# A hybrid decoder block in float32: the intra-chunk scores of a head pair issued in two runs instead of three, with the bonus product moved behind them

## The chip, the cores and the metric

The kernel runs on one core of one Trainium2 chip. The metric is the device time of one execution in microseconds (us). The core has five engines with instruction queues of their own: TensorE (PE, with its weight loads shown as PEld), VectorE (DVE), ScalarE (ACT), GpSimd (POOL) and SyncE (SP), which here only issues DMAs. Products land in PSUM, which has eight banks of 128 partitions by 512 float32.

## The reference, cut to what matters

One decoder layer over 528 positions (16 learned ones and 512 of input), 1024 channels, all in float32:

```
p   = h @ W_in                      # GLU columns | RWKV r,k,v + low-rank columns | 2 gates
A   = conv module: GLU -> causal depthwise conv(31) -> LayerNorm -> swish -> projection
Bm  = RWKV-7 time mixing (16 heads of 64) -> projection
y   = sigmoid(gA) * A + sigmoid(gB) * Bm
x   = LN(alpha * x + y @ W_o);  x = LN(alpha * x + ConvGatedMLP(x))

# RWKV-7, per head, state S (64 x 64):
S_t = S_{t-1} diag(decay_t) + (S_{t-1} a_t) b_t^T + v_t k_t^T ;  y_t = S_t r_t
o   = LN(y) + sum(r * k * r_k) * v          # the second term is the "bonus"
```

## The kernel before, in words

The recurrence is computed in 9 chunks of 64 positions (chunk 0 holds only the 16 learned positions), for two heads at a time, so that a pair of heads fills 128 partitions: head 0 lies on partitions 0 to 63, head 1 on 64 to 127. There are 8 such pairs, p = 0 to 7. For each pair the code has these stages; the string SCHEDULE writes their order by hand:

- K (`rkv`): the r, k and v columns of the input projection, 6 half-width products, each of 24 matmuls (three for each of 8 blocks, L172, L175, L176) into a bank of tag "g". ACT and DVE empty the bank (L225, L227). G (`glu`) and A (`gate`) are further such products and do not depend on the pair's recurrence.
- P (`prep`): the decays, then the two operands of the scores, AR (from r and k, L434 and L436) and BK (L437 to L470; its last step is the multiplication at L470, in two parts: chunks 0 to 4, then 5 to 8). Then the bonus: two products with a matrix of ones (L478) into two banks of tag "a", each read by DVE together with v into the tile bv (L479). Then the scores: for each chunk and each head a 128 x 128 product over that head's 64 partitions (L490). Then 8 scalings of AR in place on ACT (L498), and transposes of BK and v (L506, L510), again through banks of tag "a".
- S (`solve`): a triangular solve on DVE in 31 dependent steps (L560 to L570), fed from the scores through DMAs, with the depthwise convolution of another channel block put between the steps (L754, L762).
- C (`merge` and `chain`): the solved blocks are brought back, then the 9 chunks are run one behind the other on PE, ACT and DVE (L624, L643 to L660). F (`finish`): norm, bonus and output gate (L671 to L713); it is the last reader of bv (L704).

The scores are issued in three parts, chunk 0, chunks 1 to 4 and chunks 5 to 8. Each part takes two banks of tag "a", one for each head; DVE multiplies each bank by a causal mask into the tile Gt (L492). Each float32 product is two passes on PE, so a part of one chunk is 4 records in the trace and a part of four chunks 16.

PSUM banks are handed out by tag: "g" has 3 banks (K, G, A), "x" has 2 (chain and finish), "a" has 2 (prep), "m" has 1 (a small product of prep at L454, and two of merge at L606 and L611). A tile of a tag waits until one of the tag's banks is released by its last reader.

The order of instructions on each engine is fixed at build time by a planner that goes by priority, which is the order of the code unless a block stands in `with front()`, which gives its instructions the highest priority; `behind(b, a, why)` makes b follow a on the same engine without a semaphore. merge and chain stand in `front()`; prep does not.

The tiles AR, Gt, bv, BT and UV have two buffers each, so those of pair p become free when chain and finish of pair p-2 have read them.

Of the kernel before, what the change touches and what calls it, by code (L numbers as in the profile page):

```python
# [11 lines left out]
F32 = mybir.dt.float32  # L12
F32R = mybir.dt.float32r
AF = mybir.ActivationFunctionType
ALU = mybir.AluOpType
# [3 lines left out]
P = 128  # L19
# [7 lines left out]
NCH = 9  # L27
# [19 lines left out]
GW = 132  # L47
# [7 lines left out]
def hybrid_block(ctx: ExitStack, tc: tile.TileContext, a, out, dbg=None):  # L55
    nc = tc.nc
    V, S, G, TE = nc.vector, nc.scalar, nc.gpsimd, nc.tensor
# [5 lines left out]
    def pool(stack, name, side, **kw):  # L63
        return stack.enter_context(tc.tile_pool(name=name, bufs=1, side=side, reuse_waits="tile", **kw))

    front = tc.high_priority
# [4 lines left out]
    def behind(ins, first, why):  # L71
        tc.add_manual_dep(ins.ins, first.ins.name, mybir.DependencyInfo(mybir.DependencyClass.NoSync,
                                                                mybir.DependencyReason.DATA), reason=why)
# [8 lines left out]
    def bank(tag, bufs):  # L82
        return psp.tile([P, 512], F32, name="ps_" + tag, tag=tag, bufs=bufs)

    gbank = lambda: bank("g", 3)
    xbank = lambda: bank("x", 2)
    abank = lambda: bank("a", 2)
    mbank = lambda: bank("m", 1)
# [18 lines left out]
    cmask = cp.tile([P, P], F32, name="cmask")  # L107
# [79 lines left out]
    turn, turn_a = cycle((gbank, xbank, gbank, xbank, gbank)), cycle((gbank, abank, gbank, abank, gbank))  # L187
# [21 lines left out]
    sp = pool(ctx_a2, "scan", "left")  # L209
# [39 lines left out]
    with tc.tile_pool(name="start", bufs=1, side="right", reuse_waits="tile") as st:  # L249
# [88 lines left out]
        c0 = 43  # L338
        for i, n in ((1, 112), (2, 128), (3, 120), (4, 88), (5, 44)):
# [15 lines left out]
                    in1=taps[:, :, 1, :], op=ALU.add)  # L355
# [31 lines left out]
    def prep(p, r, k, v):  # L387
# [15 lines left out]
        for hf, (t0, t1) in enumerate(HALF):  # L403
# [9 lines left out]
            else:  # L413
# [16 lines left out]
        AR = sp.tile([P, NCH, P], F32, name="AR", bufs=2)  # L430
        BK = ra.tile([P, NCH, P], F32, name="BK", bufs=1)
# [7 lines left out]
                               in1=Ei[:, :, 1:65], op0=ALU.mult, op1=ALU.mult)  # L439
# [24 lines left out]
        for g0, g1, c0, c1 in ((0, 3, 0, 5), (3, 5, 5, NCH)):  # L464
            pt = abank()
            for i in range(g0, g1):
# [4 lines left out]
                            in1=pt[:, 0:64 * (c1 - c0)].rearrange("p (c t) -> p c t", t=64), op=ALU.mult)  # L471


        bv = sp.tile([P, NQ], F32, name="bv", bufs=2)
        for t0, t1 in QH:
            pt = abank()
# [2 lines left out]
            V.tensor_tensor(out=bv[:, t0 - Q0:t1 - Q0], in0=pt[:, :n], in1=v[:, 64 + OFF + t0:64 + OFF + t1],  # L479
                            op=ALU.mult)  # L480


        Gt = sp.tile([P, 2, NCH, GW], F32, name="Gt", bufs=2)
        G.memset(Gt.rearrange("p h c (two x) -> p (h c two) x", two=2)[:, :, 64:66], 0.0)
        for c0, c1 in ((0, 1), (1, 5), (5, 9)):
            pts = [abank(), abank()]
            for c in range(c0, c1):
                for h in range(2):
                    o = pts[h][:, P * (c - c0):P * (c - c0 + 1)]
                    TE.matmul(o, BK[64 * h:64 * h + 64, c, :], AR[64 * h:64 * h + 64, c, :], start=True, stop=True)  # L490
            for h in range(2):
                V.tensor_tensor(out=Gt[:, h, c0:c1, :].rearrange("p c (two x) -> p c two x", two=2)[:, :, :, 0:64],  # L492
                                in0=pts[h][:, 0:P * (c1 - c0)].rearrange("p (c two t) -> p c two t", two=2, t=64),
                                in1=cmask.rearrange("p (two t) -> p two t", two=2).unsqueeze(1).broadcast_to(
                                    [P, c1 - c0, 2, 64]), op=ALU.mult)

        for c in range(1, NCH):
            S.activation(out=AR[:, c, :], in_=AR[:, c, :], func=AF.Copy, scale=lc[:, c - 1:c])  # L498
# [327 lines left out]
    for step in SCHEDULE.split():  # L826
        what, p, q = step[0], int(step[1:2] or 0), int(step[2:] or -1)
        if what == "K":
            raw[p] = rkv(p)
        elif what == "P":  # L830
            prs[p] = prep(p, *raw.pop(p))
        elif what == "S":
            solved[p] = solve(prs[p], conv(q, cpads.pop(q)) if q >= 0 else ())
        elif what == "C":
            with front():
                merge(prs[p], *solved[p])
                ys[p] = chain(prs[p])
        elif what == "F":
            finish(prs[p], ys.pop(p))
        elif what == "G":  # L840
            cpads[p] = glu(p)
        elif what == "T":
            with back():
                for _ in conv(p, cpads.pop(p)):
                    pass
        elif what == "A":
            gate(gates.pop(0))
        elif what == "N":
            ctx_a1.close()
            rb, zh, zl, mean = conv_norm()  # L850
        elif what == "H":
            hold.append(mean)
# [27 lines left out]
    op = pool(ctx_o, "rout", "left")  # L880
# [119 lines left out]
    for j in range(2, NF):  # L1000
        c = j - 2
# [80 lines left out]
```

## Time and profile before

| | us |
|---|---|
| three runs: median (lowest to highest) | 1181.84 (1171.94 to 1184.82) |
| the profiled execution | 1175.08 |
| its span, first to last instruction | 1173.0 |
| PE busy / DVE busy / ACT busy in the span | 1121.2 / 862.9 / 567.5 |
| mean granted TensorE clock, share of full speed | 0.989 |

How to read the rows below: times are in us from the start of the span. An engine's busy time is the union of its instructions. In rows of the order of time, the first column is the start, the second the length, then engine, line, operation, output tile <- input tiles, shapes, and how many instructions were merged into the row. Matmuls overlap in the pipeline, so what one costs is the distance from start to start, not its length. In rows on waits, "A <- B: t, n, m" means that A's engine stood idle t us in n places, at most m at once, until B was done.

### The profile page before, as it was taken

The numbers are of one execution on the slowest core, as the hardware profiler recorded it, in microseconds if no ns is written. First come the engines' busy times: TensorE is split into PE (matmuls) and PEld (weight loads), VectorE is DVE, ScalarE is ACT, GpSimd is POOL, SyncE is SP. The second block draws the span as 40 slices with busy tenths as digits, with TensorE's granted clock in tenths as the row PEclk, the third lists the DMA queues.
The fourth block names the chain that finished last, engine by engine and source line by source line (L and its number), as shares of the span: only waits on it lengthen the run. The fifth ranks groups of instructions, "written<-read, shape, count | busy, mean of one in ns | idle before, by whom it ended". The sixth has DMA issues, their size and how long they took to land.

```text
span 1173.0 us, 22681 instructions
## 1 busy us (share of the span) xinstructions
PE 1121.2 (96%) x8718; PEld 1056.2 (90%) x8718; DVE 862.9 (74%) x2179; ACT 567.5 (48%) x1214; POOL 83.6 (7%) x242
## 2 busy tenths in 40 slices
PE   5999999999999999999987999999999999999997
PEld 4998989899898989989887999998999999998885
DVE  6598998889899998976586366697876666662228
ACT  5644456637556565665577433355434343441120
POOL 7001011101101110101000000000000000000000
PEclk9999999999999999999988999999999999999999
DMA  5333341333414143354432476531332323333321
GB/s 163 84 93 92 87 97 50 87 77 91 101 56 109 42 103 79 85 125 106 140 100 65 139 227 203 158 88 54 109 109 73 108 73 109 89 123 113 102 78 72
DMA packets 202438, 118.99 MB, mean 101 GB/s; under 512 B 50036, under 2 KB 186397, under 8 KB 202331
## 3 DMA queue, kind: packets, MB, share of 16 engines
q1 hardware_dynamic: 182992, 113.81, 34.6%
q10 hardware_dynamic: 17515, 3.17, 1.5%
q8 instruction: 68, 1.11, 0.4%
q0 software_dynamic: 1824, 0.57, 0.3%
q14 instruction: 39, 0.32, 0.1%
HBM read 102.24 MB, written 15.28 MB: 100 GB/s over the span
## 4 chain that ended last, share of the span: by engine, by line
PE 65%; DVE 7%; DMA 4%; ACT 3%; issue 2%; DVEq 0%; ACTq 0%; POOL 0%; SPq 0%; POOLq 0%
PE ps_x L624 7%; PE ps_g L175 6%; PE ps_g L176 6%; PE ps_g L172 6%; PE ps_g L182 4%; PE ps_g L183 4%; PE ps_g L184 4%; PE psf L1027 3%; PE psf L1026 3%; PE psf L1028 3%; PE ps_x L182 3%; PE ps_x L183 3%; PE ps_x L184 3%; ACT wh L153 1%; PE ps_a L490 1%
## 5 line engine op out<-in xcount | busy, mean ns | idle before, releaser
L172 PE MATMUL ps_g<-hhi,wh 128*128 128x256 f32 (+2 forms) x944 | 278.9, 296 | 2.6 <-DVE v L227 1.7
L175 PE MATMUL ps_g<-hhi,wl 128*128 128x256 f32 (+2 forms) x944 | 278.6, 295 | 0.0
L176 PE MATMUL ps_g<-hlo,wh 128*128 128x256 f32 (+2 forms) x944 | 278.0, 295 | 0.0
L154 DVE TENSOR_TENSOR wl<-wr,wh 128x1024 fp32r<-128x1024 f32 x151 | 182.6, 1220 | 96.8 <-ACT wh L153 96.5
L153 ACT CAST wh<-wr 128x1024 fp32r<-128x1024 f32 x151 | 158.2, 1049 | 128.9 <-PE psf L1027 73.4
L172 PEld LDWEIGHTS ps_g<-hhi,wh 128*128 128x128 f32 x944 | 180.5, 191 | 5.2 <-DVE v L227 2.2
L175 PEld LDWEIGHTS ps_g<-hhi,wl 128*128 128x128 f32 x944 | 180.1, 191 | 2.6 <-issue 0.6
L176 PEld LDWEIGHTS ps_g<-hlo,wh 128*128 128x128 f32 x944 | 180.3, 191 | 1.4 <-issue 0.4
L182 PE MATMUL ps_g<-hhi,wh 128*128 128x256 f32 (+1 forms) x424 | 120.0, 283 | 0.0
L183 PE MATMUL ps_g<-hhi,wl 128*128 128x256 f32 (+1 forms) x424 | 119.2, 281 | 0.4 <-DVE wl L154 0.4
L184 PE MATMUL ps_g<-hlo,wh 128*128 128x256 f32 (+1 forms) x424 | 118.9, 281 | 0.0
L762 DVE SCALAR_TENSOR_TENSOR cev<-cd,drv,cev 128x257 f32<-128x257 f32 x216 | 99.1, 478 | 0.1
L182 PE MATMUL ps_x<-hhi,wh 128*128 128x256 f32 (+1 forms) x280 | 79.0, 282 | 1.7 <-ACT hhi L138 1.7
L183 PEld LDWEIGHTS ps_g<-hhi,wl 128*128 128x128 f32 x424 | 79.7, 188 | 0.7 <-DVE wl L154 0.7
L182 PEld LDWEIGHTS ps_g<-hhi,wh 128*128 128x128 f32 x424 | 79.7, 188 | 0.3 <-ACT wh L153 0.2
L184 PEld LDWEIGHTS ps_g<-hlo,wh 128*128 128x128 f32 x424 | 79.8, 188 | 0.0
L183 PE MATMUL ps_x<-hhi,wl 128*128 128x256 f32 (+1 forms) x280 | 78.6, 281 | 0.0
L184 PE MATMUL ps_x<-hlo,wh 128*128 128x256 f32 (+1 forms) x280 | 78.5, 280 | 0.0
L624 PE MATMUL ps_x<-UV,Gt 128*66 128x64 f32 (+1 forms) x576 | 70.7, 245 | 3.4 <-DMA Gt<-dT 2.6
L624 PEld LDWEIGHTS ps_x<-UV,Gt 128*66 128x66 f32 (+1 forms) x576 | 64.9, 166 | 5.1 <-DMA Gt<-dT 2.8
L1027 PE MATMUL psf<-wh,hidl 128*128 128x512 f32 x176 | 69.3, 394 | 0.0
L1026 PE MATMUL psf<-wh,hidh 128*128 128x512 f32 x176 | 69.0, 392 | 0.0
(371 smaller groups left out, 2542.6 us busy)
## 6 DMA issues: line engine op xcount, KB each, us to landing
wr<-in_w_in_dram SPq DMA_DIRECT2D x59, 512.0 KB, 4.3
wr<-in_ffn_up_dram SPq DMA_DIRECT2D x44, 512.0 KB, 4.0
wr<-in_ffn_down_dram SPq DMA_DIRECT2D x22, 512.0 KB, 3.6
wr<-in_w_o_dram SPq DMA_DIRECT2D x10, 512.0 KB, 4.9
g_dr<-gt SPq DMA_DIRECT2D x16, 257.0 KB, 2.9
L<-dA SPq DMA_DIRECT2D x32, 128.0 KB, 4.0
wr<-in_w_conv_out_dram SPq DMA_DIRECT2D x8, 512.0 KB, 4.3
wr<-in_w_rwkv_out_dram SPq DMA_DIRECT2D x8, 512.0 KB, 6.2
```

Of the source, the lines that this page charges most:

```text
L153: first = S.copy(out=hi, in_=raw)
L154: V.tensor_tensor(out=lo, in0=raw, in1=hi.bitcast(F32), op=ALU.subtract)
L172: first = TE.matmul(ps, wh[:, k, :], xh(k, sl), start=(k == 0), stop=False)
L175: TE.matmul(ps, wl[:, k, :], xh(k, sl), start=False, stop=False)
L176: TE.matmul(ps, wh[:, k, :], xl(k, sl), start=False, stop=(k == nk - 1))
L182: TE.matmul(ps, wh[:, k, :], xh(k, sl), start=(k == 0), stop=False)
L183: TE.matmul(ps, wl[:, k, :], xh(k, sl), start=False, stop=False)
L184: TE.matmul(ps, wh[:, k, :], xl(k, sl), start=False, stop=(k == nk - 1))
L624: mm = lambda o, l, r, start: TE.matmul(o, l, r, start=start, stop=True, skip_group_check=True)
L762: yield V.scalar_tensor_tensor(out=yp[:, b, :] if lasttap else ev[:, b, :], in0=d[:, i:i + NM], scalar=dcol(D_HCW, 8 * (2 * i + b) + j), i ...
L1026: TE.matmul(acc[t][d], hidh[:, k, ts], wd[k][0][:, ds], start=(k == 0), stop=False)
L1027: TE.matmul(acc[t][d], hidl[:, k, ts], wd[k][0][:, ds], start=False, stop=False)
```

## The change

In `prep`, the scores now come ahead of the bonus product in the code. Chunk 0's two heads take one bank of tag "g" and the bank of tag "m"; chunks 1 to 4 take the two "a" banks as before, without waiting for chunk 0 to be read; chunks 5 to 8 take the "a" banks again. The score products stand in `front()`, and inside a part head 0 of a chunk is put behind head 1 of the chunk before, so that the heads alternate on PE. The masks (L492) of chunk 0 are written behind the products of chunks 1 to 4, outside `front()`. The bonus product and its multiplication follow, as they were.

```diff
+        Gt = sp.tile([P, 2, NCH, GW], F32, name="Gt", bufs=2)
+        G.memset(Gt.rearrange("p h c (two x) -> p (h c two) x", two=2)[:, :, 64:66], 0.0)
+        parts = ((0, 1), (1, 5), (5, 9))
+        score_banks = {}
+        for i, (c0, c1) in enumerate(parts):
+            pts = score_banks[i] = [gbank(), mbank()] if i == 0 else [abank(), abank()]
+            with front():
+                for c in range(c0, c1):
+                    for h in range(2):
+                        o = pts[h][:, P * (c - c0):P * (c - c0 + 1)]
+                        score = TE.matmul(o, BK[64 * h:64 * h + 64, c, :], AR[64 * h:64 * h + 64, c, :], start=True,
+                                          stop=True)
+                        if h == 0 and c > c0:
+                            behind(score, other, "the heads in turn")
+                        other = score
+            if i == 0:
+                continue
+            for i_, h in ((0, 0), (0, 1), (1, 0), (1, 1)) if i == 1 else ((2, 0), (2, 1)):
+                c0, c1 = parts[i_]
+                pts = score_banks[i_]
+                V.tensor_tensor(out=Gt[:, h, c0:c1, :]..., in0=pts[h]..., in1=cmask..., op=ALU.mult)
+
         bv = sp.tile([P, NQ], F32, name="bv", bufs=2)
         for t0, t1 in QH:
             pt = abank()
...
-        Gt = sp.tile([P, 2, NCH, GW], F32, name="Gt", bufs=2)
-        G.memset(Gt.rearrange("p h c (two x) -> p (h c two) x", two=2)[:, :, 64:66], 0.0)
-        for c0, c1 in ((0, 1), (1, 5), (5, 9)):
-            pts = [abank(), abank()]
-            for c in range(c0, c1):
-                for h in range(2):
-                    o = pts[h][:, P * (c - c0):P * (c - c0 + 1)]
-                    TE.matmul(o, BK[64 * h:64 * h + 64, c, :], AR[64 * h:64 * h + 64, c, :], start=True, stop=True)
-            for h in range(2):
-                V.tensor_tensor(out=Gt[:, h, c0:c1, :]..., in0=pts[h]..., in1=cmask..., op=ALU.mult)
```

## Rows read from the trace of the kernel before

**Rows 1.** The page, busy us of an engine (share of the span) xinstructions
```profile
PE 1121.2 (96%) x8718; PEld 1056.2 (90%) x8718; DVE 862.9 (74%) x2179; ACT 567.5 (48%) x1214; POOL 83.6 (7%) x242
```

**Rows 2.** Busy time in one stretch: us, PE, PEld, DVE, ACT, POOL, PEclk, DMA, GB/s
```profile
84.00:545.00 461.00, 449.47 (x3688) 420.74 (x3687) 413.09 (x1335) 265.07 (x646) 52.72 (x144) 0.99 0.35 85
```

**Rows 3.** Waits of PE, whole span
```profile
PE ps_g L182 <- ACT zh L138: 6.9, 1, 6.9
...
PE ps_a L802 <- DVE csum L797: 3.5, 1, 3.5
...
PE ps_a L490 <- DVE Gt L492: 0.2, 1, 0.2
```

**Rows 4.** PE in order of time around the scores of pair 0
```profile
86.77 0.28 PE L176 MATMUL ps_g<-hlo,wh 128*128 128x256 f32 x1
86.98 0.48 PE L490 MATMUL ps_a<-AR,BK 64*128 64x128 f32 x2
87.40 0.39 PE L172 MATMUL ps_g<-hhi,wh 128*128 128x256 f32 x1
87.71 0.48 PE L490 MATMUL ps_a<-AR,BK 64*128 64x128 f32 x2
88.13 0.39 PE L175 MATMUL ps_g<-hhi,wl 128*128 128x256 f32 x1
88.35 0.28 PE L176 MATMUL ps_g<-hlo,wh 128*128 128x256 f32 x1
88.47 0.28 PE L172 MATMUL ps_g<-hhi,wh 128*128 128x256 f32 x1
88.68 1.17 PE L490 MATMUL ps_a<-AR,BK 64*128 64x128 f32 x16
89.78 0.39 PE L175 MATMUL ps_g<-hhi,wl 128*128 128x256 f32 x1
...
90.47 0.28 PE L172 MATMUL ps_g<-hhi,wh 128*128 128x272 f32 x1
90.77 1.75 PE L490 MATMUL ps_a<-AR,BK 64*128 64x128 f32 x16
92.45 0.39 PE L175 MATMUL ps_g<-hhi,wl 128*128 128x272 f32 x1
```

**Rows 5.** Busy time of L490 alone by stretch: pair 0, then all pairs
```profile
84.00:94.00 10.00, 3.89 (x36) 3.13 (x36) 1.00 0.22 58
...
sum 479.00, PE 33.16 PEld 26.46; mean PE 2.21 PEld 1.76
```

**Rows 6.** DVE in order of time in pair 4
```profile
342.27 0.42 DVE L470 TENSOR_TENSOR BK<-BK,ps_a 128x256 f32<-128x256 f32 x1
...
343.64 0.75 DVE L436 TENSOR_TENSOR AR<-r,E 128x576 f32<-128x576 f32 x1
...
354.72 0.69 DVE L704 TENSOR_TENSOR on<-on,bv 128x514 f32<-128x514 f32 x1
...
355.52 0.76 DVE L712 TENSOR_TENSOR on<-ps_x,on 128x258 f32<-128x258 f32 x2
...
356.94 0.41 DVE L479 TENSOR_TENSOR bv<-ps_a,v 128x256 f32<-128x256 f32 x1
...
358.52 0.28 DVE L492 TENSOR_TENSOR Gt<-ps_a,cmask 128x128 f32<-128x128 f32 x1
...
361.43 0.69 DVE L492 TENSOR_TENSOR Gt<-ps_a,cmask 128x512 f32<-128x512 f32 x1
```

**Rows 7.** PE in order of time in pair 4
```profile
342.98 0.59 PE L478 MATMUL ps_a<-rk,bones 128*128 128x256 f32 x2
...
344.15 0.66 PE L624 MATMUL ps_x<-UV,Gt 128*128 128x64 f32 x4
...
350.95 0.29 PE L176 MATMUL ps_g<-hlo,wh 128*128 128x272 f32 x1
351.08 0.28 PE L172 MATMUL ps_g<-hhi,wh 128*128 128x256 f32 x1
...
356.04 0.42 PE L624 MATMUL ps_x<-UV,Gt 128*66 128x64 f32 x4
```

**Rows 8.** ACT in order of time in pair 4
```profile
360.91 1.28 ACT L498 ACTIVATE AR<-AR,lc 128x128 f32<-128x128 f32 x4 [1.03 <-PE ps_a L490]
365.01 0.49 ACT L225 ACTIVATE r<-ps_g,prm 128x272 f32<-128x272 f32 x1 [0.34 <-PE ps_g L176]
```

More of the change, by code (lines that the diff above doesn't have):

```diff
@@ L471, in prep @@
                             in1=pt[:, 0:64 * (c1 - c0)].rearrange("p (c t) -> p c t", t=64), op=ALU.mult)
+        Gt = sp.tile([P, 2, NCH, GW], F32, name="Gt", bufs=2)
[18 more added lines that the diff above has]
+                pts = score_banks[i_]
+                V.tensor_tensor(out=Gt[:, h, c0:c1, :].rearrange("p c (two x) -> p c two x", two=2)[:, :, :, 0:64],
+                                in0=pts[h][:, 0:P * (c1 - c0)].rearrange("p (c two t) -> p c two t", two=2, t=64),
+                                in1=cmask.rearrange("p (two t) -> p two t", two=2).unsqueeze(1).broadcast_to(
+                                    [P, c1 - c0, 2, 64]), op=ALU.mult)
         bv = sp.tile([P, NQ], F32, name="bv", bufs=2)
@@ L480, in prep @@
                             op=ALU.mult)
-        Gt = sp.tile([P, 2, NCH, GW], F32, name="Gt", bufs=2)
-        G.memset(Gt.rearrange("p h c (two x) -> p (h c two) x", two=2)[:, :, 64:66], 0.0)
-        for c0, c1 in ((0, 1), (1, 5), (5, 9)):
-            pts = [abank(), abank()]
-            for c in range(c0, c1):
-                for h in range(2):
-                    o = pts[h][:, P * (c - c0):P * (c - c0 + 1)]
-                    TE.matmul(o, BK[64 * h:64 * h + 64, c, :], AR[64 * h:64 * h + 64, c, :], start=True, stop=True)
-            for h in range(2):
[L492 to L495, printed above, removed]
         for c in range(1, NCH):
```

## The prediction, as recorded before the result was known

> **What bounds the kernel now.** I read the page's busy times first. PE is busy 1121.2 us of a span of 1173.0, DVE 862.9, ACT 567.5 [rows 1], so PE is the engine to ask about. Shares over a whole span hide stages, so next I took the stretch in which all eight head pairs are prepared, 84 to 545 us: PE 449.47 of 461.00 us, which is 97.5%, DVE 413.09, 89.6% [rows 2]. PE bounds this stretch and DVE is a near second. Third, PE's waits: the two longest that touch this case lie behind the stretch, 6.9 and 3.5 us while the convolution's norm is worked out; the wait of a score product for a bank that DVE has not yet read is 0.2 us in all [rows 3]. So the bank rounds of the scores cost PE almost nothing as *waits*. What they cost must be looked for in PE's busy time, and that is why I went to the order of time on PE.
>
> There the reader is to see the distance between starts. Full-width projection matmuls follow each other every 0.12 us (88.35 to 88.47). When one score product (two passes) is put between two of them, their distance is 0.63 us (86.77 to 87.40) and in the second case 0.73 (87.40 to 88.13). When eight products run together and the two heads alternate, the distance is 1.31 us (88.47 to 89.78). When eight run together but head 0's come first because head 1's bank is not free, it is 1.98 us (90.47 to 92.45) [rows 4]. Less the 0.12 that the projection would have taken, pair 0's scores cost 0.51 + 0.61 + 1.19 + 1.86 = 4.17 us of PE time. Entering and leaving the half-height products is dear (a lone product costs 0.51) and more of them, in turn, are cheap: a lone product is two steps (its two passes), the run of eight is eight steps of two passes, one of each head, so a step is (1.31 - 0.63) / 6 = 0.11 us.
>
> **Part by part.**
>
> *All pairs before.* L490 is busy 3.89 us in pair 0 and 33.16 in the eight pairs [rows 5]. Pair 0's cost, 4.17, is 0.28 above its busy time for four runs. Taking the same surplus for all, the eight pairs cost 33.2 + 8 x 0.28 = 35.4 us, 4.4 each.
>
> *After, if it goes as written.* Chunk 0 joins chunks 1 to 4: ten products, two steps more than the run of eight, 1.31 + 0.22 - 0.12 = 1.41 us. Chunks 5 to 8 in turn: 1.19. Together 2.60 us for a pair, a saving of 1.8, or 14.6 us for eight. This is the upper bound of the saving on PE.
>
> *After, if both runs are split.* The "a" banks come free one after the other: L470 reads the transposed norms in two steps, and the masks of 512 columns take 0.69 us each [rows 6], against steps of 0.11 on PE. If the planner starts head 0 as soon as its bank is free and fills with projections until head 1's is, the first run becomes two: three products, of which head 0 has two (four steps, 0.51 + 0.22), and seven (still eight steps for head 1, 1.19), 1.92 us; the second a lone product and seven, 0.51 + 1.19 = 1.70. A pair then costs 3.62, a saving of 0.8, or 6.4 us for eight. I take between: L470's two parts follow each other within the time of three products, so the first run will often be whole, 1.6; the masks are longer, so the second will mostly be split, 1.6. Together 3.2 us, a saving of 1.22 a pair, 9.8 us for eight.
>
> *Masks, bonus, memset.* The same 48 masks, 16 bonus multiplications and 16 bonus products with the same shapes; no DMA is added. The masks of chunk 0 now stand in one group with those of chunks 1 to 4: 2 x 0.28 + 2 x 0.69 = 1.94 us on DVE [rows 6] before both "a" banks are free for the third part. PE has independent projections for that time, as it has now (waits of 0.2 us [rows 3]); if that cover were gone, 1.94 us would be lost in each pair. The page TensorEngine Tiling (Array Packing) of the Trainium skill, section Performance Considerations, PSUM Bottleneck, warns of just this: tiling makes TensorE faster but not the emptying of PSUM. By it the third part would go at DVE's pace and its pairing would be worth nothing; rows 3 show no such wait in this kernel, and it is the second rival below.
>
> *The move of the bonus.* In pair 4 the bonus took both "a" banks at 342.98 [rows 7], and DVE could read them only when finish of pair 2 had let go of bv at 354.72; it did so until 357.35. The scores' operands were complete at 344.39 (L436) [rows 6]. So the scores stood 13 us behind banks that the bonus held, and the same pattern holds in pairs 5, 6 and 7; in pairs 0 to 3 the bonus was read at once. With the scores first, they start near 344.4 there, behind the last chain product that reads the old AR (344.15 [rows 7]). What is late next: the solve of the pair before is still on DVE, so the solve starts no earlier; ACT's eight scalings of AR, which stood waiting for the scores with the emptying of r behind them (r's half ended on PE at 351.2, ACT emptied it at 365.01 [rows 7, 8]), come sooner. PE was full meanwhile, so I put the direct gain at 0 and leave what may come of it to a rival.
>
> *High priority, and the two borrowed banks.* The scores now go ahead of chain products, about 3 us a pair, and chain's steps have projections beside them; 0. The bank of tag "m" lies idle between prep and merge in the trace's order; 0. The bank of tag "g" is one of three that the projections live on. Banks seem to be granted in the order of the code: chain of pair 3, high in priority, began at 356.04 only when finish's first "x" bank had been read (L712, from 355.52), though chain's previous product had started at 344.15 [rows 6, 7]. If so, the "g" bank is kept from the place where prep stands in the code, long before the scores, and projections have two. A half takes 24 x 0.125 = 3.0 us (350.95 to 351.08 is one step [rows 7]); two banks suffice as long as a half is emptied within 3 us. I take 0.1 us a pair, 0.8 us in all, between 0 and the price of the third rival.
>
> Sum: 9.8 - 0.8 = 9 us on PE, and PE passes it on: DVE needs 413 us of what would then be 452, 91%. 1175.08 - 9 = 1166.1 for the profiled execution. That one was 0.6% below the median of the runs shown (1181.84), so 1181.84 x 1166.1 / 1175.08 = 1172.8.
>
> **The rivals** (times on the median's footing, x 1.0058).
>
> First, chunk 0 still goes alone. Its two banks are of other tags, so it need not wait for "a" banks; in pairs where "a" is late it runs by itself, 0.63 + 0.01 - 0.12 = 0.52 us, and eight products follow. A pair costs 0.52 + 1.19 + 1.70 = 3.4, or 3.9 if that run is split too: a saving of 0.5 to 1.0, 6 us for eight, 1176. For it: separate tags, separate readiness. Against it: in four pairs the last operand is AR, by which time "a" is free.
>
> Second, PE stands still for the masks: the scores head PE's queue and the third part waits there for 1.94 us of masks. 8 x 1.94 = 15.5 against 14.6 saved: 1183, no change. For it: high priority. Against it: rows 3.
>
> Third, the other side: the "g" bank. A half of r ended at 351.2 and was emptied 13.8 us later [rows 7, 8]. Behind such a half PE can fill two more banks now, 6 us of work, and only one if the scores' bank is kept; 3 us are lost at each such place. With 9 saved, one such place in each pair gives -9 + 24 = 15 us, 1190, or 1197; seven places are the point of slower by 1%. Against it: in pairs 4 to 7 the earlier scores free that bank, and ACT, before r is due.
>
> Fourth, more than PE's time is saved: earlier scores in four pairs bring the last pair's solve and the norm forward, and half of the 10.4 us of idle there [rows 3] goes too: -14, 1161, or 1168.
>
> **How the numbers follow.** Forecast as summed, 0.50, its own range 1167 to 1178 (savings of 14.6 and of some 4); chunk 0 alone 0.12; masks 0.11; the "g" bank 0.13; the fourth 0.14. One per cent, about what a measurement of this kernel can tell from no change, is 11.8 us, so faster means below 1170.0: the fourth and 0.20 of the forecast's 0.50, 0.34. Slower is the third, 0.13. Within 1% is the rest, 0.53. The range takes in the fourth with some more and the second, and leaves out the third: 1160 to 1188.
>
> **What would show it.** Right: L490 busy falls from 33.2 to between 20 and 28 us, in two or three runs a pair; in pairs 4 to 7 scores start some 13 us earlier against L436 than against L479 now; PE's waits for L492 stay under 2 us. Wrong: new PE waits in front of L172 on ACT or DVE readers of "g" (third), in front of L490 (second), four-record runs of L490 by themselves (first), or a span that does not follow PE's busy time down.

## The result and the profile after

| | before | after |
|---|---|---|
| median of the runs, us (lowest to highest) | 1181.03 (four runs, beside after's) | 1304.83 (1295.38 to 1307.86, four runs) |
| span of the profiled execution, us | 1173.0 | 1304.4 |
| PE busy in the span, us | 1121.2 | 1143.6 |
| PE idle in the span, us (span less busy) | 51.8 | 160.8 |
| mean granted TensorE clock | 0.989 | 0.922 |

The changed kernel is slower by a tenth: ratio 1.103, interval 1.0985 to 1.1074. Of the 131.4 us that the span grew by, 109.0 are idle of PE and 22.4 are more busy time of PE for the same 8718 records, which goes with the lower clock. First the page of after: busy time by engine, against [rows 1], and the slices for PE's busy share and granted clock (40 slices, tenths).

```profile
PE 1143.6 (88%) x8718; PEld 1074.1 (82%) x8718; DVE 882.0 (68%) x2179; ACT 576.6 (44%) x1216; POOL 85.0 (7%) x242
...
PE   5979399499597979299499999999899999999997
...
PEclk9979599699796989579789999999999999999999
```

The holes (idle stretches of PE) lie in the first half of the span, where the head pairs are prepared, and about one in each pair. The stretch of [rows 2] in after (us, PE, PEld, DVE, ACT, POOL, PEclk, DMA, GB/s):

```profile
84.00:545.00 461.00, 367.71 (x2878) 339.95 (x2878) 351.31 (x1115) 220.04 (x536) 47.95 (x128) 0.85 0.25 63
```

PE was busy 449.47 us there and is now busy 367.71; it gets through 2878 records in place of 3688. PE's waits in after, whole span, tell at which instruction it stands:

```profile
PE ps_a L468 <- ACT nsb L462: 104.5, 8, 22.4
PE ps_g L486 <- DVE BK L470: 7.3, 8, 2.3
```

Eight waits, one in each pair, 104.5 us in sum: nearly all of the 109.0. L468 is the transposes of the norms, an instruction that the change doesn't touch. In before the same group of instructions waited for the same releaser 0.4 us (columns: busy us, mean ns, idle before and its releaser):

```profile
L468 PE MATMUL ps_a<-ident,nsb 128*128 128x128 f32 (+1 forms) x40 | 7.3, 267 | 0.4 <-ACT nsb L462 0.4
```

So the norm isn't the news; in before, something else ran while it was worked out. What is missing is seen in the order of time on PE in pair 1 of after (start us, length, engine, line, output <- inputs, shapes, count, idle before):

```profile
127.06 0.28 PE L176 MATMUL ps_g<-hlo,wh 128*128 128x256 f32 x1
...
127.68 1.12 PE L454 MATMUL ps_m<-e,sq 128*66 128x2 f32 x10
...
129.99 0.28 PE L418 MATMUL ps_a<-lap,wul 128*128 128x256 f32 x1
152.66 1.64 PE L468 MATMUL ps_a<-ident,nsb 66*128 66x66 f32 x5 [22.39 <-ACT nsb L462]
154.45 0.58 PE L486 MATMUL ps_g<-AR,BK 64*128 64x128 f32 x1 [0.15 <-DVE BK L470]
154.46 0.58 PE L486 MATMUL ps_m<-AR,BK 64*128 64x128 f32 x1
...
155.25 1.71 PE L486 MATMUL ps_a<-AR,BK 64*128 64x128 f32 x14
157.01 1.89 PE L619 MATMUL ps_m<-t11n,a 128*128 128x32 f32 x8
158.71 0.57 PE L172 MATMUL ps_g<-hhi,wh 128*128 128x272 f32 x1
```

No projection matmul (L172, L175, L176) runs from 127.06 until the scores have begun at 154.45 in their "g" bank; the next one starts at 158.71. All three "g" banks stood empty for most of that time. Their last readers are done before 129, on ACT and on DVE in the order of time of after:

```profile
127.38 0.47 ACT L225 ACTIVATE r<-ps_g,prm 128x255 f32<-128x255 f32 x1 [2.33 <-PE ps_g L176]
```

```profile
128.37 0.49 DVE L227 SCALAR_TENSOR_TENSOR r<-ps_g,drv,r 128x256 f32<-128x256 f32 x1
```

In every pair of after the order is the same: all projections that stand ahead of this pair's prep in the code run, then PE waits, then the scores begin, then the projections that stand behind prep. In before they ran far ahead of the scores (in pair 1, all 10 halves of K2 and G2, which stand behind prep in the code, were through by 150.7 us, and the scores began at 156.8). What the wait does to the clock shows in PE's windows of after around it (stretch, its length, PE's busy time, granted clock, DMA share, GB/s):

```profile
130.00:152.00 22.00, 0.27 (x2) 0.53 0.15 43
152.00:164.00 12.00, 10.99 (x59) 0.50 0.23 36
164.00:176.00 12.00, 11.28 (x91) 0.94 0.32 67
```

In 130 to 152 us PE is busy for 0.27 us at a clock that is already down to 0.53 in the mean, and the 12 us behind it run at a granted clock of 0.50, the 1.2 GHz level: there the idle costs a second time.

### The profile page after: what moved, and what is told of

Same layout as the page of the kernel before. It is cut to its first block, busy times and chain, and to the rows that moved or that the text cites. A ratio compares the mean times of both kernels' runs of the same rounds, so it can differ in the third digit from the quotient of the medians.

```text
span 1304.4 us, 22692 instructions
## 1 busy us (share of the span) xinstructions
PE 1143.6 (88%) x8718; PEld 1074.1 (82%) x8718; DVE 882.0 (68%) x2179; ACT 576.6 (44%) x1216; POOL 85.0 (7%) x242
## 4 chain that ended last, share of the span: by engine, by line
PE 69%; DVE 19%; DMA 5%; ACT 4%; issue 2%; SPq 0%; ACTq 0%; DVEq 0%
PE ps_g L172 8%; PE ps_g L175 8%; PE ps_g L176 8%; PE ps_x L637 7%; DVE cev L775 5%; PE ps_g L183 4%; PE ps_g L182 4%; PE ps_g L184 4%; PE psf L1040 3%; PE psf L1039 3%; PE ps_x L182 3%; PE psf L1041 3%; PE ps_x L183 3%; PE ps_x L184 3%; PE ps_a L486 3%
## 5 line engine op out<-in xcount | busy, mean ns | idle before, releaser
L172 PE MATMUL ps_g<-hhi,wh 128*128 128x256 f32 (+2 forms) x944 | 280.2, 297 | 0.1
L175 PE MATMUL ps_g<-hhi,wl 128*128 128x256 f32 (+2 forms) x944 | 277.2, 294 | 0.0
L176 PE MATMUL ps_g<-hlo,wh 128*128 128x256 f32 (+2 forms) x944 | 276.7, 293 | 0.0
L172 PEld LDWEIGHTS ps_g<-hhi,wh 128*128 128x128 f32 x944 | 181.2, 192 | 2.5 <-issue 2.0
L175 PEld LDWEIGHTS ps_g<-hhi,wl 128*128 128x128 f32 x944 | 181.2, 192 | 0.7 <-issue 0.5
L176 PEld LDWEIGHTS ps_g<-hlo,wh 128*128 128x128 f32 x944 | 180.6, 191 | 0.6 <-issue 0.2
L468 PE MATMUL ps_a<-ident,nsb 128*128 128x128 f32 (+1 forms) x40 | 11.9, 421 | 105.6 <-ACT nsb L462 104.5
L468 PEld LDWEIGHTS ps_a<-ident,nsb 128*128 128x128 f32 (+1 forms) x40 | 7.2, 210 | 109.0 <-ACT nsb L462 106.3
```

The lines of the kernel that those rows point to most:

```text
L172: first = TE.matmul(ps, wh[:, k, :], xh(k, sl), start=(k == 0), stop=False)
L175: TE.matmul(ps, wl[:, k, :], xh(k, sl), start=False, stop=False)
L176: TE.matmul(ps, wh[:, k, :], xl(k, sl), start=False, stop=(k == nk - 1))
```

## The experiments

Seen from this, the theory is **A**: the banks of one tag are granted in the order in which the code asks for them. The scores' "g" bank is asked for where prep stands; until the scores' operands are there, every later request of the tag is behind it, though banks are empty. Against it: **B**, the high priority and the turns hold projections back; **C**, projections are merely short of one bank in three; **D**, the bonus product behind the scores does it. Each kernel was measured beside runs of before of its own (medians 1175 to 1179 us), so ratios are what to compare. "By starts" is the prediction's way to price the scores: the distance from the start ahead of each run of scores to the start behind it, less the 0.12 us of one projection matmul, summed over the runs.

**Chunk 0 back in "a" banks, all else as changed.**

```diff
-            pts = score_banks[i] = [gbank(), mbank()] if i == 0 else [abank(), abank()]
+            pts = score_banks[i] = [abank(), abank()]
...
-            if i == 0:
-                continue
-            for i_, h in ((0, 0), (0, 1), (1, 0), (1, 1)) if i == 1 else ((2, 0), (2, 1)):
+            for i_, h in ((i, 0), (i, 1)):
```

> The changed kernel, but with chunk 0's two banks taken from tag "a" again and its masks written right behind its products; high priority, the heads in turn and the bonus behind the scores stay. Theory A (banks of a tag go out strictly in the order of the code, so that no projection written behind prep gets a "g" bank before chunk 0's scores have theirs): PE's wait of 104.5 us at L468 falls under 10 us and the time comes back to 1165 to 1185 us, the saving on the scores showing at most as 1%. Theory B (high priority or the heads in turn make PE's order wait): the wait stays, 1290 to 1305 us. Theory C (the projections lack one of three banks) agrees with A here. Theory D (the bonus behind the scores holds something up): the wait stays, about 1300 us.

1167.88 us, ratio 0.9916 (0.9887 to 0.9945). The wait at L468 is 0.7 us, and the time lies in A's range. Priority, turns and the bonus's place are all still there, so B and D don't make the loss.

**Chunk 0's first bank under a tag of its own, "g" cut to two banks.**

```diff
-    gbank = lambda: bank("g", 3)
+    gbank = lambda: bank("g", 2)
+    sbank = lambda: bank("s", 1)
...
-            pts = score_banks[i] = [gbank(), mbank()] if i == 0 else [abank(), abank()]
+            pts = score_banks[i] = [sbank(), mbank()] if i == 0 else [abank(), abank()]
```

> The changed kernel, but chunk 0's first head takes a bank of a tag of its own, and tag "g" is left with two banks for the whole kernel. Theory A (the queue of tag "g" is closed by a tile that is not ready): no tile of prep stands in that queue, so PE's wait at L468 is gone, under 10 us, and the time is 1170 to 1200 us, depending on what two banks cost. Theory C (the third bank is what the projections miss): they have two banks all the time, so it is at least as slow as the changed kernel, 1290 us or more. Theory B: 1290 to 1305.

1168.55 us, ratio 0.9926 (0.9891 to 0.9960), a little below the range given for A. This is the telling one: the projections have two banks for good, and the loss is gone, with 0.4 us of wait before the norm's transposes (L469 here):

```profile
PE ps_a L469 <- ACT nsb L463: 0.4, 1, 0.4
```

C alone falls; what cost 104.5 us was the place in the queue, not the bank. It also shows what the change was to do. PE in order of time in pair 1 of this kernel:

```profile
154.95 0.28 PE L177 MATMUL ps_g<-hlo,wh 128*128 128x256 f32 x1
155.16 0.37 PE L487 MATMUL ps_s<-AR,BK 64*128 64x128 f32 x1
...
155.48 1.07 PE L487 MATMUL ps_a<-AR,BK 64*128 64x128 f32 x16
156.48 0.39 PE L173 MATMUL ps_g<-hhi,wh 128*128 128x256 f32 x1
```

Ten products in turn, start to start 1.53 us (154.95 to 156.48), 1.41 more than one projection matmul.

**Before, with the two borrowed banks alone.**

```diff
-            pts = [abank(), abank()]
+            pts = [gbank(), mbank()] if c0 == 0 else [abank(), abank()]
```

> The kernel before with one edit: chunk 0's scores take one bank of tag "g" and the bank of tag "m". The bonus stays ahead of the scores, nothing has high priority and the heads are not ordered. Theory A: the whole loss appears, 1280 to 1310 us, with PE waiting about 100 us at the norm's transposes (L468). Theories B and D: 1170 to 1185, no change. Theory C: slower too, so it is told from A by the run with a tag of its own.

1316.33 us in the profiled run, 1.117 times the 1178.86 of before beside it (a second run took 1340.47, too few for an interval), a little more than A's range. No turns, no high priority, the bonus ahead as before, and the wait is back, in PE's waits of this kernel:

```profile
PE ps_a L468 <- ACT nsb L462: 112.9, 8, 24.7
```

With these three A is shown: the borrowed banks alone make the loss, and without the request for the "g" bank the rest of the change doesn't (the "m" bank by itself is the next run).

**Chunk 0 in one "a" and the "m" bank.**

```diff
-            pts = score_banks[i] = [gbank(), mbank()] if i == 0 else [abank(), abank()]
+            pts = score_banks[i] = [abank(), mbank()] if i == 0 else [abank(), abank()]
```

> The changed kernel with chunk 0's first head in an "a" bank in place of the "g" bank; its second head stays in the "m" bank, the masks stay behind those of the next run, turns, priority and bonus stay as changed. Theory A: nothing of "g" is held, so no wait over 5 us in sum before the norm's transposes, and the time is that of the other kernels with the bonus behind, 1164 to 1174 us. The runs of scores can't join, since the third "a" request waits for the first to be emptied: 36 us for the scores. Rival E (the "m" bank, which the merge and the norm of the pairs share, closes as well): waits of TensorE before the merge's and the norm's products in "m" of over 20 us in sum and a time above 1190 us.

1166.06 us, ratio 0.9917 (0.9899 to 0.9935), with 1.6 us of wait at L468. PE's waits before products in the "m" bank of the merge are 8.2 us, against 2.9 in before and over 20 as E has it; the time shows nothing of them, so the "m" bank was rightly put at 0, and E falls. The runs did join in part (six records, then fourteen), and the scores cost 31.2 us of PE by starts, less than expected.

**The request moved behind the next projections.** The second half of prep, from the scores on, becomes a step Q; its instructions keep the priority that they had.

```diff
+        elif what == "Q":
+            rest, at = rests.pop(p)
+            with tc.high_priority(offset=tc.cur_priority - at):
+                prs[p] = rest()
...
-SCHEDULE = ("G0 K0 P0 T0 G1 S01 K1 P1 C0 K2 F0 G2 S12 K3 P2 C1 G3 F1 K4 S23 G4 P3 C2 F2 A S34 K5 P4 C3 F3 G5 S4 A "
+SCHEDULE = ("G0 K0 P0 T0 G1 Q0 S01 K1 P1 C0 K2 F0 G2 Q1 S12 K3 P2 C1 G3 F1 K4 Q2 S23 G4 P3 C2 F2 A Q3 S34 K5 P4 C3 F3 "
```

> The changed kernel with the same banks, products, turns and high priority, but the second half of prep (from the scores on) is a step of its own, Q, that stands in the list of steps behind the next pair's projections (behind G2 for pair 1, and so on); its instructions keep the priority they had at the old place. So the "g" bank of chunk 0 is asked for behind the projections that fill the wait for the norm, not ahead of them. Theory A (the banks of one tag are granted in the order in which the code asks for them, so one tile that isn't ready closes the tag): the eight waits of TensorE of 104.5 us before the norm's transposes fall under 5 us in sum, the granted clock is back at 0.98 or more, and the time is 1160 to 1172 us: the 1168 of the run with the bonus product moved alone, less what is left of the shorter scores. Rival (only the number of free "g" banks counts, two for the projections while chunk 0 holds the third): the bank is held as long as before once it is granted, so the waits stay above 60 us and the time above 1240 us. If it lies between, with other waits of TensorE named, the new order of the banks "a" and "m" costs something of its own.

1206.56 us, ratio 1.0281 (1.0251 to 1.0312). The waits before the transposes fell from 104.5 to 12.7 us, so the rival that counts free banks (above 60 us) falls, but A's under 5 us wasn't reached, the clock was 0.963 in place of 0.98, and the time was 35 us over what I expected of it. PE's waits at that line (L469 here):

```profile
PE ps_a L469 <- ACT nsb L463: 10.9, 5, 4.4
...
PE ps_a L469 <- ACT nsb L464: 1.8, 3, 1.3
```

The trace shows where the rest is. The request is no longer ahead of these projections, but it is ahead of the next ones, and where the projections run out before the operands come, the tag is closed all the same. PE in order of time in pair 5, then the windows of that stretch:

```profile
415.98 0.28 PE L177 MATMUL ps_g<-hlo,wh 128*128 128x256 f32 x1
...
425.81 0.58 PE L488 MATMUL ps_g<-AR,BK 64*128 64x128 f32 x1
...
432.09 0.57 PE L173 MATMUL ps_g<-hhi,wh 128*128 128x272 f32 x1
```

```profile
404.00:416.50 12.50, 12.50 (x105) 12.03 (x103) 8.21 (x25) 9.86 (x27) 1.40 (x7) 1.00 0.50 123
416.50:426.00 9.50, 6.94 (x38) 5.51 (x39) 7.76 (x16) 7.83 (x19) 2.37 (x7) 0.62 0.31 76
426.00:444.00 18.00, 18.00 (x97) 16.05 (x97) 8.98 (x28) 4.84 (x15) 1.54 (x3) 0.54 0.19 46
...
416.50:418.80 2.30, 1.15 (x9) 0.97 (x8) 2.28 (x6) 2.28 (x5) 0.14 (x1) 1.00 0.28 42
418.80:442.70 23.90, 22.48 (x112) 19.48 (x113) 13.51 (x35) 9.97 (x27) 3.77 (x9) 0.50 0.19 47
```

No projection is issued from 416 to 432. PE is idle for only 2.6 us of 416.5 to 426.0, 1.15 of them before the clock falls at 418.8, and the 18 us behind run at 0.54 with PE busy throughout: 97 records, where the 12.5 us ahead held 105. A small hole cost more by the clock than by itself, and so it is in the whole: against the own-tag kernel the span is 37.5 us longer (1201.5 less 1164.0), of which 24.8 are more busy time of PE (1140.6 less 1115.8) and 12.7 idle. That Q also moved prep's "a" and "m" requests is not told apart by this run.

**The bonus product moved, alone.** The bonus block of before, unchanged, stands behind the scores' block.

```diff
-        bv = sp.tile([P, NQ], F32, name="bv", bufs=2)
-        for t0, t1 in QH:
-            pt = abank()
...
         Gt = sp.tile([P, 2, NCH, GW], F32, name="Gt", bufs=2)
...
+        bv = sp.tile([P, NQ], F32, name="bv", bufs=2)
+        for t0, t1 in QH:
+            pt = abank()
...
```

> The kernel before with one edit: the bonus products and their multiplications are written behind the scores; chunk 0 keeps its "a" banks, nothing has high priority. Theory A: no stall, 1165 to 1185 us; in pairs 4 to 7 the scores start about 13 us earlier, and if that is worth something of its own it shows here as up to 1%. Theory D: about 1300 us.

1168.27 us, ratio 0.9921 (0.9897 to 0.9945): as fast as the best of the others, with scores that cost 37.1 us of PE, no less than the 36.6 of before (both by starts). So the gain that several kernels share comes with this move. In pair 5 of before, DVE and PE in order of time:

```profile
406.27 0.75 DVE L436 TENSOR_TENSOR AR<-r,E 128x576 f32<-128x576 f32 x1
...
418.11 0.70 DVE L704 TENSOR_TENSOR on<-on,bv 128x514 f32<-128x514 f32 x1
...
420.68 0.42 DVE L479 TENSOR_TENSOR bv<-ps_a,v 128x258 f32<-128x258 f32 x1
```

```profile
395.88 0.65 PE L478 MATMUL ps_a<-rk,bones 128*128 128x256 f32 x2
...
421.83 0.49 PE L490 MATMUL ps_a<-AR,BK 64*128 64x128 f32 x2
```

AR is complete at 407.02, but both "a" banks hold the bonus until DVE may write bv, behind finish's L704, at 420.68; the scores begin at 421.83. With the bonus behind (L436 on DVE, the scores at L481 on PE):

```profile
402.84 0.75 DVE L436 TENSOR_TENSOR AR<-r,E 128x576 f32<-128x576 f32 x1
```

```profile
403.64 0.49 PE L481 MATMUL ps_a<-AR,BK 64*128 64x128 f32 x4
```

From the end of L436 to the first score, pairs 5, 6 and 7 took 14.8, 15.4 and 13.6 us in before and 0.1, 3.7 and 0.5 us here. (In pairs 4 and 6 here the last operand was BK, L470 ending at 351.02 and 471.67; the scores began at 351.95 and 471.93.) The scores of pair 7 begin at 530.8 in place of 552.5, and its chain ends at 641.4 in place of 661.5. Behind the projections PE then finds work sooner, 545 to 700 us of before and of this kernel:

```profile
545.00:700.00 155.00, 140.88 (x1149) 133.04 (x1148) 93.57 (x254) 87.36 (x193) 5.38 (x15) 0.96 0.48 140
```

```profile
545.00:700.00 155.00, 146.17 (x1187) 139.23 (x1186) 95.81 (x254) 82.94 (x184) 3.59 (x11) 0.97 0.52 147
```

5.3 us of the 8.3 by which the span is shorter are idle of PE that went here; of the waits of 6.9 and 3.5 us before the convolution's norm [rows 3] neither is among its eleven longest waits.

**Turns and high priority alone, the bonus ahead; and turns alone.** The first is this edit in before; the second is the same without `with front()`.

```diff
+            with front():
...
-                    TE.matmul(o, BK[64 * h:64 * h + 64, c, :], AR[64 * h:64 * h + 64, c, :], start=True, stop=True)
+                        score = TE.matmul(o, BK[64 * h:64 * h + 64, c, :], AR[64 * h:64 * h + 64, c, :], start=True,
+                                          stop=True)
+                        if h == 0 and c > c0:
+                            behind(score, other, "the heads in turn")
+                        other = score
```

> The kernel before with the heads' turns and the high priority of the scores alone; the banks and the bonus product's place are those of before. Theory F (the whole gain of the kernels at 1168 us comes from the bonus product's move): no change, 1176 to 1181 us, and the idle of TensorE in 545 to 700 us stays at 14 us. Rival G (the scores placed earlier by any means give the same gain, by priority too): 1168 us, ratio 0.992, and that idle at 9 us, as with the bonus moved.

> The kernel before with the heads' turns alone: no high priority, the bonus product and the banks as before. The same with high priority was slower, ratio 1.0133. Theory J (the high priority of the scores made that loss): no change here, ratio 0.997 to 1.003, 1172 to 1179 us. Rival K (the order of the heads in turn made it, by delaying the first head's masks until both heads' products are through): the ratio stays near 1.013.

Both priced: 1190.81 us, ratio 1.0133 (1.0117 to 1.0150), and 1180.62 us, 1.0040 (1.0025 to 1.0056). Neither gives anything by itself, so G falls and F is right that the gain is the bonus's; but F had no change here, and the high priority made a loss of 1%: K falls, and J holds but for the 0.4% of the turns, just above its range. PE is busy 135.13 us in 545 to 700 with both, 137.22 with turns alone, 140.88 in before. The scores themselves stayed at 37.1 and 37.7 us. Why priority costs here and not in the kernels with the bonus behind was not settled.

**The price of the third "g" bank.** The kernel with the bonus moved alone, and the kernel with chunk 0 in "a" banks, each with one edit more:

```diff
-    gbank = lambda: bank("g", 3)
+    gbank = lambda: bank("g", 2)
```

> The kernel before with the bonus product moved behind the scores and the projections' tag "g" cut from three banks to two; the eighth bank is left unused. It is the kernel of the bonus move with the bank count of the kernel that gave chunk 0 a tag of its own, without the shorter scores. Theory H (the third "g" bank is what the own tag paid for its shorter scores): time 1171 to 1176 us on this footing, some 4 to 5 us above the bonus move with three banks, and TensorE's idle in 84 to 545 us at 16 us or more instead of 12.3. Rival I (two banks suffice, the shorter scores are worth nothing because something else sets the end): the ratio stays at 0.992 and that idle at 12 to 13 us. The third rival of the prediction, 3 us lost at each of eight places, would be 24 us more, 1190 us or above.

> The kernel of the run with chunk 0 in "a" banks (turns, high priority, bonus behind), with the tag "g" cut to two banks and the eighth bank left unused. It stands between the run with the bonus moved and two "g" banks (ratio 1.008, 36.0 us of TensorE for the scores) and the run with chunk 0's own tag and two "g" banks (0.993, 30.0 us). Theory L (the joined run of the own tag made up for the third "g" bank): ratio 1.004 to 1.012, some 1180 to 1189 us. Rival M (turns and high priority made it up): 0.990 to 0.996, some 1164 to 1171 us.

1183.95 us, ratio 1.0080 (1.0044 to 1.0116), and 1175.77 us, 0.9971 (0.9948 to 0.9994). Against the same kernels with three banks (0.9921 and 0.9916) the third bank is worth 1.6% and 0.55%, some 19 and 6 us; H's 1171 to 1176 us was too low a time and I's no change is out. Without the closed tag a missing bank is thus dear, but a fifth or less of what the closed tag cost. The own-tag kernel, with two banks as well, is at 0.9926; of the 1.5% between it and 1.0080, 1.1% came with turns and priority (to 0.9971), which gave nothing with three banks (0.9916 against 0.9921) and cost 1.3% in before; why isn't settled. The other 0.45% would be the joined run and its shorter scores (30.0 us against 37.6 in the middle one), some 5 us, but these two intervals overlap. So neither L nor M is confirmed.

**The bonus ahead, in a bank of its own.**

```diff
-    gbank = lambda: bank("g", 3)
+    gbank = lambda: bank("g", 2)
+    sbank = lambda: bank("s", 1)
...
-            pt = abank()
+            pt = sbank()
```

> The kernel before, the bonus product still ahead of the scores, but in one bank of its own tag, with "g" cut to two banks. Theory N (the bonus kept the scores waiting through the two "a" banks that it held until DVE had v and bv): in pairs 4 to 7 the scores start within 3 us of the end of the multiplication that completes AR, in place of 13 to 15 us, and the time is that of the bonus moved behind with two "g" banks, ratio 1.004 to 1.012. Rival O (the order on the engines held them, DVE's bonus multiplication ahead of the masks): the first scores start early, but their masks stay behind the bonus multiplication by the same 13 to 15 us, the third run of scores comes no earlier, and the time is that of the kernel before or above the other, ratio 1.012 or more.

1179.34 us, ratio 1.0001 (0.9973 to 1.0029). In pairs 5 and 6 the scores begin 0.8 and 1.1 us behind AR, in place of 14.8 and 15.4, with the bonus read 12.2 and 7.5 us later; DVE and PE in pair 5 (AR L437, bonus L480, scores L491):

```profile
406.10 0.75 DVE L437 TENSOR_TENSOR AR<-r,E 128x576 f32<-128x576 f32 x1
...
419.86 0.42 DVE L480 TENSOR_TENSOR bv<-ps_s,v 128x258 f32<-128x258 f32 x1
```

```profile
407.62 0.49 PE L491 MATMUL ps_a<-AR,BK 64*128 64x128 f32 x4
```

There it was the held banks, as N has it. In pairs 4 and 7 the scores still began 8.0 and 16.8 us behind AR, but there AR wasn't the last operand: BK was. DVE and PE in pair 4, then in pair 7 (BK L471):

```profile
357.45 0.48 DVE L471 TENSOR_TENSOR BK<-BK,ps_a 128x320 f32<-128x320 f32 x1
```

```profile
358.14 0.49 PE L491 MATMUL ps_a<-AR,BK 64*128 64x128 f32 x2
```

```profile
556.03 0.49 DVE L471 TENSOR_TENSOR BK<-BK,ps_a 128x320 f32<-128x320 f32 x1 [0.69 <-PE ps_a L469]
```

```profile
557.56 0.48 PE L491 MATMUL ps_a<-AR,BK 64*128 64x128 f32 x2
```

Behind the operand that came last, the scores of pairs 4 to 7 begin 0.2, 0.8, 0.4 and 1.0 us later, where before had 12.7 to 15.4. So the held banks are shown as what kept the scores; why BK came late in two pairs isn't settled. The time doesn't follow either theory: 1.0001 lies below N's 1.004 to 1.012 and far below O's 1.012, and it is below the 1.0080 of the bonus behind with the same two banks. With two "g" banks the bonus ahead in a bank of its own is thus the faster of the two, and these runs don't say why.

## Why the prediction was wrong

- **The step that failed is the price of the "g" bank**, "I take 0.1 us a pair, 0.8 us in all". The sentence ahead of it was right: banks are granted in the order of the code, and a chain product that stood behind an unread bank had shown it [rows 6, 7]. Its consequence was drawn for the bank ("the projections have two") and not for the queue (the projections have none until the scores are ready). The price is what PE has to wait between the last projection ahead of prep and the last operand, 13.1 us a pair (104.5 / 8), plus the slow clock behind it, not 3 us a place. The sign that the prediction named for this bank, new waits in front of L172, didn't come: the waits stood in front of L468. The third rival, 1197, had the right tag and the right direction, but it counted banks too; a missing bank by itself was measured at some 19 and 6 us, not its 24. What was put against it (scores that free the bank earlier) touches the bank, not the queue.
- **The cover was priced by the state of before.** "PE has independent projections for that time" held for the masks only as long as projections may take banks. PE's wait for L490 of 0.2 us [rows 3] was read as cheap; the right question was which work filled PE in prep, and which tag it needs.
- **The cost of the scores** was worked out well in its parts: ten in turn were put at 1.41 us, and 1.41 is what the own-tag kernel shows. The sum was short by waits: 3.2 us a pair was taken, and 30.0 / 8 = 3.75 measured there; 3.3 us of the 30.0 are waits for masks and 0.7 one for BK, and without them it is 3.25 a pair. The second part was split in all pairs, the first in one. In after itself the scores were dearer, 51.9 us by starts, 7.3 of them waits for BK (L486 <- L470) and most of the rest at the low clock behind each wait; their busy time, which was to fall to between 20 and 28 us, rose to 40.5 (in the own-tag kernel it fell to 24.8).
- **The bonus's move at 0** was wrong too, upwards. The 13 us of held banks were read rightly, and the fourth rival said what would come of them, 14 us saved in all; moved alone it gave 0.79%, some 9 us. What the sum booked as the gain of the change (9.8 us of PE) and what it booked at 0 are the other way round as far as these runs tell: with three "g" banks, the kernels with 31 to 36 us of scores are no faster than the one with 37.1.
- **The second rival** (PE stands for the masks) didn't come. In the own-tag kernel PE waited 3.3 us in sum for masks, in five places, 1.1 at the longest, against 15.5 as priced. The PSUM Bottleneck section of the Trainium skill's page TensorEngine Tiling (Array Packing), that emptying may become the limit (it speaks of a fourfold speedup of TensorE), is not borne out here at that price. **The first** (chunk 0 alone) didn't come either: it ran in the head of the joined run.
- **DVE as a near second** (91%) wasn't put to the test in after, where it fell with PE to 351.31 us of 461. In the own-tag kernel DVE was busy 420.45 us of that stretch, 91%, and PE 444.66.

No kernel is shown to beat the simplest: the bonus behind, nothing else (0.9921). Between it and the others at 0.9916 to 0.9926 these runs can't tell.

## What to carry to other kernels

A buffer that is borrowed from a busy tag is paid for from the place where the code asks for it, not from where it is filled: ask which requests of the tag stand behind it and when its own operands will be ready, and give it a tag of its own if they come late; asking later took most of the waits away here, but left the kernel 2.8% slower than before. A product that can be read only late should not hold banks ahead of one whose operands are ready. When an engine is 97% busy, look up which work fills it in each stage and what that work needs, before counting its cover as safe.

## What was not expected of the hardware

A hole in PE's work was paid about one and a fifth times here, by the granted clock: 109.0 us of idle came with 22.4 us more busy time for the same records. In pair 1 of after the run of scores (L486 from 154.45 to the merge at 157.01) took 2.56 us at a clock of 0.50, where the own-tag kernel did the same ten products in 1.32 us (155.16 to 156.48) at full clock. It needed no long hole. In the run with the later request PE was busy 1.15 of the 2.30 us ahead of the fall at 418.8, and the clock stayed at 0.50 until 442.7, with PE busy 22.48 of those 23.90 us. A like hole in before cost far less:

```profile
105.00:113.60 8.60, 5.99 (x50) 5.50 (x49) 6.24 (x16) 2.34 (x5) 1.53 (x3) 1.00 0.60 166
113.60:117.00 3.40, 3.40 (x18) 3.40 (x18) 3.32 (x13) 0.67 (x3) 0.12 (x1) 0.50 0.03 10
117.00:121.00 4.00, 4.00 (x36) 4.00 (x36) 2.24 (x5) 2.33 (x5) 0.00 (x0) 1.00 0.00 0
```

There 2.6 us of idle were followed by 3.4 us at 0.50. What makes the low clock last in one place and not in the other isn't settled by these runs.
